# Attention of a two-layer decoder trunk: values become the weights of the product, key blocks are merged by the mask, the steps stand at other slots

## The chip, the cores and the metric

The kernel runs on one core of one Trainium2 chip. TensorE (PE) multiplies; a product loads one operand as weights (PEld) and streams the other past them, and the result lands in PSUM. VectorE (DVE), ScalarE (ACT) and GpSimd (POOL) work element by element; SyncE (SP) issues most DMAs. The metric is the device time of one execution in microseconds (us), lower is better.

## The reference, cut to what matters

Two layers work on 256 tokens of width 2048. In each, the normalised input is projected to queries, keys, values, u and v of a gating unit, and gate logits. The attention branch looks back over 127 earlier tokens, in blocks of 128:

```python
q_pos = jnp.arange(BLOCK)[:, None] + BLOCK
k_pos = jnp.arange(2 * BLOCK)[None, :]
diff = q_pos - k_pos
band = (diff >= 0) & (diff < WINDOW)          # WINDOW = BLOCK = 128
valid = (jnp.arange(nb)[:, None, None] > 0) | (k_pos >= BLOCK)[None]
...
scores = jnp.where(mask, scores, -1e30)
...
probs = jax.nn.softmax(jnp.concatenate([scores, sink], axis=-1), axis=-1)[..., :-1]
out = jnp.einsum('bnhgqk,bnkhd->bnqhgd', probs.astype(v.dtype), vw)
```

There are 16 query heads and 4 key heads (each serves 4 query heads), of 64 numbers each. A query at place i of its block sees of the block before only the keys at places above i, and of its own block only the keys up to i: each place counts in exactly one of the two blocks, so a query has 128 valid keys at most. The attention output is multiplied by `w_attn_branch`, the gating unit's by `w_sgu_branch`; both are gated, merged, multiplied by `w_out` and added to x, and a SwiGLU of width 5632 follows.

## The kernel before, in words

All large products are of one form. A chunk of weights, 256 rows by 512 columns, is loaded by SP into a `raw` buffer (five of them), ACT rounds it to `whi` (line 225), DVE subtracts to `wlo` (line 226), and PE takes three products for each pair of blocks, written to `acc` (lines 314 and 315). So a weight in fp32 goes through PE in parts that PE streams in one pass. Weights are rounded and subtracted four chunks ahead of PE.

The program is a list of such chunks. `tick()` moves a counter of slots on by one for each chunk or so (12 products of `acc`). `after(n, fn)` puts a step n slots later. PE's order is as written; the order on the other engines is arranged when the program is built.

The attention of a layer is in the class `Attention`. It runs between those products, while the projection is still going on:

- `keys` and `queries` normalise and rotate, and turn the result by DVE transposes of 32x32 blocks (`turn`, line 383), whose pieces SP then gathers by 16 DMAs of 32 KB (line 388).
- `scores(t, g)` (line 723) takes one block of 128 queries `t` and one key head `g`. It makes four products of 64 rows, in two PSUM tiles, for 128 keys (t = 0) or 256 keys (t = 1). DVE adds the mask (line 727), takes the maximum, ACT takes the exponential with the sum of each row.
- `weights(t, g)` (line 752), 5 slots later, turns the probabilities by PE, four transposes for each block of keys, and ACT takes them out of PSUM (line 754).
- `values(t, g)` (line 762), 3 slots later, takes the turned probabilities as the weights and streams 64 columns of values past them, for each head and each block of keys. DVE multiplies by the reciprocal of the sum (line 766) into `att`.
- `transposed` turns `att` in the way of `turn` (16 DMAs on SP) and splits it in two parts, `uh` and `ul`, for the product with `w_attn_branch`.

The scores of the first four heads-and-blocks stand 17, 22, 27 and 32 slots behind their queries, those of the second four at 29, 34, 39 and 44. PSUM tiles named `at` are two in number; scores (two tiles), values (one) and the gating unit's mixing product (`psg`, line 840) share them. Two more, `tr`, serve the transposes.

The gating unit's `v` (class `Spatial`) gets a GELU, its means taken off and is scaled, in steps from 1 to 9 slots behind each of its two chunks.

Of the kernel before, what the change touches and what calls it, by code (L numbers as in the profile page):

```python
# [15 lines left out]
NT = 2  # L16
# [41 lines left out]
def hybrid_trunk(ctx: ExitStack, tc: tile.TileContext, x, mix_norm, w_in, q_norm, k_norm, sinks,  # L58
# [92 lines left out]
    plans = []  # L151
    for l in range(DEPTH):
        wl = w_in[l]

        def of_in(kind, c):
            o = {"kv": O_KV, "q": 0, "v": O_V, "u": O_U, "gate": O_GATE}[kind] + c * CW
            return wl[:, o:o + CW]

        for f in FIRST_PART[l]:
            plans.append((single if len(f) == 1 else pair)(("in", l), *(of_in(*c) for c in f)))  # L160
        plans += [single(("att", l), w) for w in cols_of(w_attn_branch[l], NCH)]
# [26 lines left out]
    class Stream:  # L188
# [7 lines left out]
        def load(self, upto):  # L196
            while self.asked < min(upto, len(entries)):
                for key, w, h, tag in entries[self.asked]["loads"]:
                    raw = wraw.tile([P, 2, CW], F32, tag=tag, name=nm("raw"), bufs=None if tag == "raw" else 1)
                    src = w[2 * h * P:2 * (h + 1) * P, :].rearrange("(k p) n -> p k n", p=P)  # L200
                    if self.raws:
                        self.loaded = nc.sync.dma_start(raw, src)
                    else:
                        for i in range(2):
                            self.loaded = nc.sync.dma_start(raw[:, i:i + 1], src[:, i:i + 1])
                    self.raws[key] = raw
                self.asked += 1

# [317 lines left out]
    for c in range(NCH):  # L526
# [1 line left out]
    after(7, lambda: norm.finish())  # L528
    after(10, lambda: norm.unit(WINO, again=True))

    mask = const.tile([P, S], F32, name="mask")
    nc.gpsimd.memset(mask, 0.0)
    nc.gpsimd.affine_select(mask[:, :P], mask[:, :P], pattern=[[1, P]], base=0, channel_multiplier=-1,
                            compare_op=ALU.is_gt, fill=-1e30)
    nc.gpsimd.affine_select(mask[:, P:], mask[:, P:], pattern=[[-1, P]], base=0, channel_multiplier=1,
                            compare_op=ALU.is_ge, fill=-1e30)
    cs = const.tile([P, NT, HD // 2], F32, name="cs")
    sn = const.tile([P, NT, HD // 2], F32, name="sn")
    nc.gpsimd.dma_start(cs, cosine.rearrange("(t p) h -> p t h", p=P))
# [92 lines left out]
    def fetch_large(pl):  # L632
        for n, i in ((13, 2), (17, 3), (21, 0), (25, 1)):
            after(n, lambda i=i: pl.fetch(i))
        after(40, pl.spatial)

    class Attention:


        def __init__(self, pl):  # L640
            self.pl = pl
            self.qT = [None] * 2
            self.att = [None] * 2
            self.attT = [None] * 2
            self.live = {}

        def rotate(self, src, n, rope, outs):

# [35 lines left out]
        def keys(self, kv):  # L684
# [2 lines left out]
            self.rotate(kv[:, :, :KVW], NKV, self.pl.rope[1], [kd[:, :, :, j, :] for j in range(2)])  # L687
            self.kT = slot([P, 4, NKV, NT, B], name="kT")
            after(K_TURN, lambda: turn(self.kT, kd.rearrange("p t n a d -> p t (n a d)"), nc.sync))

        def queries(self, c, q):
            self.rotate(q, NQ // 2, self.pl.rope[0], None)
            self.qT[c] = slot([P, 4, S], name="qT")
            self.att[c] = slot([P, NT, CW], name="att")
# [18 lines left out]

        def scores(self, t, g):
            nk = P * (t + 1)
            mk = mask[:, P:] if t == 0 else mask
            snk, nsnk = self.pl.snk, self.pl.nsnk
            pr = slot([P, 2, 2, S], name="pr")
            for j in range(2):
                pscore = ps_at.tile([P, 2, S], F32, tag="at", name=nm("psc"))  # L720
                for i in range(2):
# [5 lines left out]
                nc.vector.tensor_tensor(out=pr[:, :, j, :nk], in0=pscore[:, :, :nk],  # L727
                                        in1=mk.unsqueeze(1).to_broadcast([P, 2, nk]), op=ALU.add)
            pr4 = pr.rearrange("p i j k -> p (i j) k")
            mx = tiny(4, "mx")  # L730
            nc.vector.tensor_reduce(out=mx, in_=pr4[:, :, :nk], axis=AX.X, op=ALU.max)
# [5 lines left out]
            nc.scalar.activation(es, es, AF.Exp)  # L737
            den = tiny(4, "den")
            for h in range(4):
                nc.scalar.activation(pr4[:, h, :nk], pr4[:, h, :nk], AF.Exp, bias=nm_[:, h:h + 1],  # L740
                                     accum_out=den[:, h:h + 1])
# [3 lines left out]
            after(5, lambda: self.weights(t, g, pr4, rd))  # L745

        def weights(self, t, g, pr4, rd):
            pT = []
            for kb in range(t + 1):
                pt = ps_tr.tile([P, 4, P], F32, tag="tr", name=nm("ppt"))  # L750
                for h in range(4):
                    nc.tensor.transpose(pt[:, h, :], pr4[:, h, kb * P:(kb + 1) * P], ident)  # L752
                pT_ = temp((P, 4, P), "pT")
                nc.scalar.activation(pT_, pt, AF.Copy)
                pT.append(pT_)
            after(3, lambda: self.values(t, g, pT, rd))

        def values(self, t, g, pT, rd):
            po = ps_at.tile([P, 4, HD], F32, tag="at", name=nm("po"))
            for h in range(4):  # L760
                for kb in range(t + 1):
                    nc.tensor.matmul(po[:, h, :], pT[kb][:, h, :],  # L762
                                     self.kv[:, kb, KVW + g * HD:KVW + (g + 1) * HD],
                                     start=kb == 0, stop=kb == t)
            o = (g % 2) * 256
            nc.vector.tensor_tensor(out=self.att[g // 2][:, t, o:o + 256].rearrange("p (h d) -> p h d", d=HD),
                                    in0=po, in1=rd.unsqueeze(2).to_broadcast([P, 4, HD]), op=ALU.mult)

    class Spatial:

# [236 lines left out]
```

## Time and profile before

| what | value |
| --- | --- |
| median of 3 runs | 2474.78 us (2472.15 to 2475.66) |
| the profiled execution | 2473.06 us |
| its span in the profile | 2471.1 us |
| busy: PE, PEld, DVE, ACT, POOL | 99%, 82%, 78%, 58%, 11% |
| granted clock of TensorE | 1.00 |
| DMA, mean | 203 GB/s |

The page gives busy time per engine, the chain of work that ended last, and the costliest groups of instructions (line, engine, operation, tile written and read, shape, count, busy time, mean duration of one, idle time before and what ended it). A matmul's duration includes its way through the array, so that durations of neighbours overlap: what a product costs is read from the distance between starts in the timeline. An fp32 product that isn't split appears as two instructions of PE, a transpose as one.

### The profile page before, as it was taken

What the parts mean: (1) busy time and instruction counts of PE and PEld (TensorE: products, weight loads), DVE (VectorE), ACT (ScalarE), POOL (GpSimd) and SP (SyncE); (2) the same over time, 40 slices, a digit from 0 to 9 for tenths busy, and PEclk for the clock granted to TensorE, in tenths of its full rate; (3) what the DMA queues carried; (4) which work ended last, traced back from release to release, by engine and by line L of the source; (5) the groups of instructions that cost most, each with busy time, mean ns of one, the idle gap of its engine ahead of it and who ended that gap; (6) DMA issues with size and microseconds to landing.
All of it is one profiled execution on the core that took longest, in us unless ns stands there. A gap on an engine that the chain in (4) does not pass through costs nothing.

```text
span 2471.1 us, 31179 instructions
## 1 busy us (share of the span) xinstructions
PE 2456.6 (99%) x11088; PEld 2032.1 (82%) x11088; DVE 1925.3 (78%) x2261; ACT 1430.8 (58%) x1794; POOL 283.2 (11%) x527
## 2 busy tenths in 40 slices
PE   9999999999999999999999999999999999999999
PEld 7888888888888888888887888888888888888887
DVE  6798676887877787778887986767878777877786
ACT  5566544575655565556655665545655555655564
POOL 3100002231110111011101000021211001110110
PEclk9999999999999999999999999999999999999999
DMA  9655667576766667576757546666767566666664
GB/s 293 203 181 163 214 200 218 182 241 190 220 197 204 214 195 223 175 228 188 227 153 265 154 155 224 208 209 188 231 188 233 189 215 195 218 198 202 213 196 148
DMA packets 275662, 502.54 MB, mean 203 GB/s; under 512 B 26225, under 2 KB 36049, under 8 KB 275505
## 3 DMA queue, kind: packets, MB, share of 16 engines
q1 hardware_dynamic: 259472, 484.25, 61.8%
q0 software_dynamic: 15712, 16.01, 2.2%
q8 instruction: 87, 1.43, 0.2%
q14 instruction: 71, 0.57, 0.1%
q10 hardware_dynamic: 320, 0.27, 0.0%
HBM read 475.27 MB, written 2.10 MB: 193 GB/s over the span
## 4 chain that ended last, share of the span: by engine, by line
PE 94%; DVE 2%; DMA 1%; SPq 1%; issue 1%; ACT 0%; POOL 0%; DVEq 0%; ACTq 0%
PE acc L314 61%; PE acc L315 30%; DMA raw<-in_w_in_dram 1%; SPq L388 1%; DVE wlo L226 1%; PE po L762 1%; PE pt L425 1%; PE ppt L752 0%; PE psc L723 0%; ACT whi L225 0%; PE psg L840 0%; DVE box L383 0%; POOL rq L286 0%; DVE raw L213 0%; DVE gate L928 0%
## 5 line engine op out<-in xcount | busy, mean ns | idle before, releaser
L226 DVE TENSOR_TENSOR wlo<-raw,whi 128x1024 fp32r<-128x1024 f32 (+1 forms) x1039 | 1260.7, 1219 | 493.7 <-ACT whi L225 485.1
L225 ACT ACTIVATE whi<-raw 128x1024 fp32r<-128x1024 f32 (+1 forms) x1039 | 1098.2, 1058 | 919.4 <-PE acc L315 720.9
L314 PE MATMUL acc<-whi,uh 128*128 128x512 f32 x3114 | 1217.9, 391 | 1.2 <-ACT uh L411 1.2
L314 PE MATMUL acc<-wlo,uh 128*128 128x512 f32 x3114 | 1214.0, 390 | 2.2 <-DVE wlo L226 2.2
L315 PE MATMUL acc<-whi,ul 128*128 128x512 f32 x3114 | 1213.5, 390 | 0.0
L314 PEld LDWEIGHTS acc<-wlo,uh 128*128 128x128 f32 x3114 | 585.1, 188 | 124.9 <-DVE wlo L226 5.0
L314 PEld LDWEIGHTS acc<-whi,uh 128*128 128x128 f32 x3114 | 585.1, 188 | 121.7 <-ACT uh L411 1.8
L315 PEld LDWEIGHTS acc<-whi,ul 128*128 128x128 f32 x3114 | 584.9, 188 | 121.7 <-DVE ul L416 0.2
L388 POOL DMA_DIRECT2D tt<-box x480 | 235.2, 497 | 1714.9 <-DVE box L383 784.1
L213 DVE TENSOR_TENSOR raw<-raw,raw 128x1024 f32<-128x1024 f32 x188 | 229.2, 1219 | 1.3
L314 PE MATMUL acc<-whi,sh 128*128 128x512 f32 x376 | 147.3, 392 | 0.0
L314 PE MATMUL acc<-wlo,sh 128*128 128x512 f32 x376 | 147.1, 391 | 0.0
L315 PE MATMUL acc<-whi,sl 128*128 128x512 f32 x376 | 146.5, 390 | 0.0
L315 PEld LDWEIGHTS acc<-whi,sl 128*128 128x128 f32 x376 | 70.6, 188 | 14.7
L314 PEld LDWEIGHTS acc<-wlo,sh 128*128 128x128 f32 x376 | 70.7, 188 | 14.6 <-DVE kept L339 0.4
L314 PEld LDWEIGHTS acc<-whi,sh 128*128 128x128 f32 x376 | 70.7, 188 | 14.3
L339 DVE TENSOR_TENSOR kept<-acc,kept 128x512 f32<-128x512 f32 x94 | 64.2, 684 | 0.0
L342 ACT ACTIVATE acc<-kept 128x512 f32<-128x512 f32 x94 | 55.1, 587 | 10.8 <-DVE kept L339 10.7
L857 DVE SCALAR_TENSOR_TENSOR xs<-acc,xs 128x512 f32<-128x512 f32 (+1 forms) x66 | 41.4, 666 | 7.8 <-PE acc L315 7.8
L946 ACT ACTIVATE hid<-acc,rhalf 128x512 f32<-128x512 f32 x44 | 30.4, 690 | 21.0 <-PE acc L315 21.0
L947 DVE SCALAR_TENSOR_TENSOR hid<-hid,acc 128x512 f32<-128x512 f32 x44 | 29.6, 683 | 8.3 <-ACT hid L946 8.3
L336 ACT ACTIVATE kept<-acc 128x512 f32<-128x512 f32 x47 | 28.0, 597 | 13.2 <-PE acc L315 13.2
(135 smaller groups left out, 880.5 us busy)
## 6 DMA issues: line engine op xcount, KB each, us to landing
raw<-in_w_in_dram SPq DMA_DIRECT2D x239, 512.0 KB, 4.7
raw<-in_w_up_dram SPq DMA_DIRECT2D x176, 512.0 KB, 4.8
raw<-in_w_gate_dram SPq DMA_DIRECT2D x176, 512.0 KB, 4.3
raw<-in_w_down_dram SPq DMA_DIRECT2D x176, 512.0 KB, 4.6
raw<-in_w_out_dram SPq DMA_DIRECT2D x64, 512.0 KB, 4.8
raw<-in_w_attn_branch_dram SPq DMA_DIRECT2D x32, 512.0 KB, 5.3
raw<-in_w_sgu_branch_dram SPq DMA_DIRECT2D x32, 512.0 KB, 4.3
tt<-box POOLq DMA_DIRECT2D x480, 32.0 KB, 4.2
```

The source lines that it names most:

```text
L213: self.last = nc.vector.tensor_tensor(out=self.raws[d], in0=self.raws[x], in1=self.raws[y], op=ALU.subtract)
L225: nc.scalar.activation(hi[:, i, :], raw[:, i, :], AF.Copy)
L226: self.last = nc.vector.tensor_tensor(out=lo[:, i, :], in0=raw[:, i, :], in1=hi[:, i, :].bitcast(F32), op=ALU.subtract)
L314: nc.tensor.matmul(ps, a, part[:, kk, :], start=first and kk + n == 0, stop=False, skip_group_check=True)
L315: nc.tensor.matmul(ps, b, hi[:, kk, :], start=False, stop=kk == 1, skip_group_check=True)
L336: nc.scalar.activation(p.kept[:, 1, :], a[0], AF.Copy)
L339: nc.vector.tensor_tensor(out=p.kept[:, int(tag == "P7"), :], in0=a[1], in1=p.kept[:, 1, :], op=ALU.add)
L342: nc.scalar.activation(ps, p.kept[:, t, :], AF.Copy)
L388: queue.dma_start(dst[j * B:(j + 1) * B, i], box[i * B:(i + 1) * B, j])
L857: nc.vector.scalar_tensor_tensor(out=xs[:, t, sl], in0=sums[t][:, i * w:(i + 1) * w], scalar=scale, in1=xs[:, t, sl], op0=ALU.mult, op1=AL ...
L946: nc.scalar.activation(th, g[t], AF.Tanh, scale=norm.rh[t])
L947: nc.vector.scalar_tensor_tensor(out=th, in0=th, scalar=1.0, in1=g[t], op0=ALU.add, op1=ALU.mult)
```

## The change

- `scores`: the block of 256 keys becomes 128. For t = 1 ACT copies the scores of the own block, and DVE writes the scores of the block before over them where the mask says so (`copy_predicated`). Maximum and exponential work on 128 keys. The buffer `pr` is of another pool (five buffers that it shares with short-lived work of the GELU and others).
- The probabilities are multiplied by the reciprocal of their sum on DVE, 4 slots behind the scores, 128x512 at a time.
- `weights`: four transposes for either t, 7 slots behind the scores. For t = 1 DVE makes a second copy in which only the keys of the own block are kept (`causal`).
- `values(t, c)`: one step for two key heads. The values are the weights (64 columns), and 512 columns of probabilities stream past them; the two key heads write to partitions 0 to 63 and 64 to 127. For t = 1 the two products of a head are: all probabilities with the values of the block before, and the kept ones with the difference of the two blocks' values, which DVE makes once per layer. The result has the channels in the partitions already: ACT and DVE split it into `uh` and `ul` straight out of PSUM, and `att`, its DVE transposes and its DMAs are gone.
- The rows of `w_attn_branch` are loaded in the order in which the heads now lie: two DMAs over 64 partitions in the place of one over 128.
- Slots: scores at 15, 19, 23, 27 and 31, 36, 41, 46; values 10 slots behind the second score of their pair; the second `v` chunk's GELU and scaling 10 slots later; the transposes of the spatial weights at slot 34 in the place of 40.

```diff
-Q_FIRST = 17
-Q_STEP = 5
+W_TURN = 7
+V_LATE = 0, 10
+SCORES = (15, 19, 23, 27), (31, 36, 41, 46)
...
+    def rows_of(raw, w, h):
+
+        if w.shape[0] != QW or not any(w is a for a in by_heads):
+            return [(raw, w[2 * h * P:2 * (h + 1) * P, :].rearrange("(k p) n -> p k n", p=P))]
+        rows = w.rearrange("(c a k d) n -> c a d k n", c=2, a=2, d=HD)
+        k = 2 * (h % 2)
+        return [(raw[a * HD:(a + 1) * HD], rows[h // 2, a, :, k:k + 2]) for a in range(2)]
...
-        after(40, pl.spatial)
+        after(34, pl.spatial)
...
+            after(K_TURN, lambda: nc.vector.tensor_tensor(out=kv[:, 0, :KVW], in0=kv[:, 1, KVW:], in1=kv[:, 0, KVW:],
+                                                          op=ALU.subtract))
...
-            n = Q_FIRST + (4 * Q_STEP - 8) * c
             for t in range(NT):
-                for g in (2 * c, 2 * c + 1):
-                    after(n, lambda t=t, g=g: self.scores(t, g))
-                    n += Q_STEP
-            after(n + 6, lambda: transposed(self.attT, c, self.att[c], queue=nc.sync))
+                for i in range(2):
+                    after(SCORES[c][2 * t + i], lambda t=t, g=2 * c + i: self.scores(t, g))
+                after(SCORES[c][2 * t + 1] + W_TURN + 3, lambda t=t: self.values(t, c))
...
-                nc.vector.tensor_tensor(out=pr[:, :, j, :nk], in0=pscore[:, :, :nk],
-                                        in1=mk.unsqueeze(1).to_broadcast([P, 2, nk]), op=ALU.add)
+                mk = mask.unsqueeze(1).to_broadcast([P, 2, P])
+                if t == 0:
+                    nc.vector.tensor_tensor(out=pr[:, :, j, :], in0=pscore[:, :, :P], in1=mk, op=ALU.add)
+                else:
+                    nc.scalar.activation(pr[:, :, j, :], pscore[:, :, P:], AF.Copy)
+                    nc.vector.copy_predicated(pr[:, :, j, :], mk.bitcast(mybir.dt.uint32), pscore[:, :, :P])
...
+            after(4, lambda: nc.vector.tensor_tensor(out=pr4, in0=pr4, in1=rd.unsqueeze(2).to_broadcast([P, 4, P]),
+                                                     op=ALU.mult))
+            after(W_TURN, lambda: self.weights(t, g, pr4))
...
-            for h in range(4):
-                for kb in range(t + 1):
-                    nc.tensor.matmul(po[:, h, :], pT[kb][:, h, :],
-                                     self.kv[:, kb, KVW + g * HD:KVW + (g + 1) * HD],
-                                     start=kb == 0, stop=kb == t)
...
+            po = ps_at.tile([P, 4, P], F32, tag="at", name=nm("po"))
+            pT = self.pT[t, c]
+            for k in range(t + 1):
+                for a in range(2):
+                    v = (1 - k) * KVW + (2 * c + a) * HD
+                    nc.tensor.matmul(po[a * HD:(a + 1) * HD], self.kv[:, 0, v:v + HD], pT[k][:, a],
+                                     start=k == 0, stop=k == t)
+            uh, ul = (x[:, :, t * P:(t + 1) * P] for x in units)
+            nc.scalar.activation(uh, po, AF.Copy)
+            nc.vector.tensor_tensor(out=ul, in0=po, in1=uh.bitcast(F32), op=ALU.subtract)
...
-                after(1 + t, lambda t=t: self.gelu(vt, t))
-                after(4 + 3 * t, lambda t=t: self.center(c, t))
+                after(V_LATE[c] + 1 + t, lambda t=t: self.gelu(vt, t))
+                after(V_LATE[c] + 4 + 3 * t, lambda t=t: self.center(c, t))
```

More of the change, by code (lines that the diff above doesn't have):

```diff
@@ L149, in pair @@
         return Plan(key, head, body)
-    plans = []
+    plans, by_heads = [], []
     for l in range(DEPTH):
@@ L160, in hybrid_trunk @@
             plans.append((single if len(f) == 1 else pair)(("in", l), *(of_in(*c) for c in f)))
-        plans += [single(("att", l), w) for w in cols_of(w_attn_branch[l], NCH)]
+        by_heads += cols_of(w_attn_branch[l], NCH)
+        plans += [single(("att", l), w) for w in by_heads[-NCH:]]
         sgu = [single(("sgu", l), w_sgu_branch[l, :, j * CW:(j + 1) * CW]) for j in range(NCH)]
@@ L199, in load @@
                     raw = wraw.tile([P, 2, CW], F32, tag=tag, name=nm("raw"), bufs=None if tag == "raw" else 1)
[L200 to L205, printed above, removed]
+                    for dst, src in rows_of(raw, w, h):
+                        if self.raws:
+                            self.loaded = nc.sync.dma_start(dst, src)
+                        else:
+                            for i in range(2):
+                                self.loaded = nc.sync.dma_start(dst[:, i:i + 1], src[:, i:i + 1])
                     self.raws[key] = raw
@@ L529, in hybrid_trunk @@
     after(10, lambda: norm.unit(WINO, again=True))
-    mask = const.tile([P, S], F32, name="mask")
+    mask = const.tile([P, P], F32, name="mask")
     nc.gpsimd.memset(mask, 0.0)
-    nc.gpsimd.affine_select(mask[:, :P], mask[:, :P], pattern=[[1, P]], base=0, channel_multiplier=-1,
-                            compare_op=ALU.is_gt, fill=-1e30)
-    nc.gpsimd.affine_select(mask[:, P:], mask[:, P:], pattern=[[-1, P]], base=0, channel_multiplier=1,
+    nc.gpsimd.affine_select(mask, mask, pattern=[[-1, P]], base=0, channel_multiplier=1,
                             compare_op=ALU.is_ge, fill=-1e30)
+    causal = const.tile([P, P], F32, name="causal")
+    nc.gpsimd.memset(causal, 1.0)
+    nc.gpsimd.affine_select(causal, causal, pattern=[[1, P]], base=0, channel_multiplier=-1, compare_op=ALU.is_ge, fill=0.0)
     cs = const.tile([P, NT, HD // 2], F32, name="cs")
@@ L642, in __init__ @@
             self.qT = [None] * 2
-            self.att = [None] * 2
             self.attT = [None] * 2
-            self.live = {}
+            self.pT, self.out = {}, {}
         def rotate(self, src, n, rope, outs):
@@ L693, in queries @@
             self.qT[c] = slot([P, 4, S], name="qT")
-            self.att[c] = slot([P, NT, CW], name="att")
+            self.attT[c] = None
             after(Q_TURN, lambda: self.turn_queries(c, q))
-            n = Q_FIRST + (4 * Q_STEP - 8) * c
             for t in range(NT):
-                for g in (2 * c, 2 * c + 1):
-                    after(n, lambda t=t, g=g: self.scores(t, g))
-                    n += Q_STEP
-            after(n + 6, lambda: transposed(self.attT, c, self.att[c], queue=nc.sync))
+                for i in range(2):
+                    after(SCORES[c][2 * t + i], lambda t=t, g=2 * c + i: self.scores(t, g))
+                after(SCORES[c][2 * t + 1] + W_TURN + 3, lambda t=t: self.values(t, c))
         def turn_queries(self, c, q):
@@ L715, in scores @@
             nk = P * (t + 1)
-            mk = mask[:, P:] if t == 0 else mask
             snk, nsnk = self.pl.snk, self.pl.nsnk
-            pr = slot([P, 2, 2, S], name="pr")
+            pr4 = temp((P, 4, P), "pr")
+            pr = pr4.rearrange("p (i j) k -> p i j k", j=2)
             for j in range(2):
@@ L726, in scores @@
                                      start=True, stop=True)
[L727 to L729 removed]
+                mk = mask.unsqueeze(1).to_broadcast([P, 2, P])
+                if t == 0:
+                    nc.vector.tensor_tensor(out=pr[:, :, j, :], in0=pscore[:, :, :P], in1=mk, op=ALU.add)
+                else:
+                    nc.scalar.activation(pr[:, :, j, :], pscore[:, :, P:], AF.Copy)
+                    nc.vector.copy_predicated(pr[:, :, j, :], mk.bitcast(mybir.dt.uint32), pscore[:, :, :P])
             mx = tiny(4, "mx")
[L731 removed]
+            nc.vector.tensor_reduce(out=mx, in_=pr4, axis=AX.X, op=ALU.max)
             nm_ = tiny(4, "negm")
@@ L744, in scores @@
             nc.vector.reciprocal(out=rd, in_=den)
-            after(5, lambda: self.weights(t, g, pr4, rd))
-        def weights(self, t, g, pr4, rd):
-            pT = []
-            for kb in range(t + 1):
-                pt = ps_tr.tile([P, 4, P], F32, tag="tr", name=nm("ppt"))
-                for h in range(4):
[L752 to L756, printed above, removed]
@@ L758, in values @@
-        def values(self, t, g, pT, rd):
-            po = ps_at.tile([P, 4, HD], F32, tag="at", name=nm("po"))
-            for h in range(4):
-                for kb in range(t + 1):
-                    nc.tensor.matmul(po[:, h, :], pT[kb][:, h, :],
-                                     self.kv[:, kb, KVW + g * HD:KVW + (g + 1) * HD],
-                                     start=kb == 0, stop=kb == t)
-            o = (g % 2) * 256
-            nc.vector.tensor_tensor(out=self.att[g // 2][:, t, o:o + 256].rearrange("p (h d) -> p h d", d=HD),
-                                    in0=po, in1=rd.unsqueeze(2).to_broadcast([P, 4, HD]), op=ALU.mult)
+            after(4, lambda: nc.vector.tensor_tensor(out=pr4, in0=pr4, in1=rd.unsqueeze(2).to_broadcast([P, 4, P]),
+                                                     op=ALU.mult))
@@ new lines, in scores, with weights @@
+            after(W_TURN, lambda: self.weights(t, g, pr4))
+        def weights(self, t, g, pr4):
+            if g % 2 == 0:
+                self.pT[t, g // 2] = [slot([P, 2, 4, P], name="pT") for _ in range(t + 1)]
+            pT = self.pT[t, g // 2]
+            pt = ps_tr.tile([P, 4, P], F32, tag="tr", name=nm("ppt"))
+            for h in range(4):
+                nc.tensor.transpose(pt[:, h, :], pr4[:, h, :], ident)
+            nc.scalar.activation(pT[0][:, g % 2], pt, AF.Copy)
+            if t == 1:
+                nc.vector.tensor_tensor(out=pT[1][:, g % 2], in0=pt, in1=causal.unsqueeze(1).to_broadcast([P, 4, P]),
+                                        op=ALU.mult)
@@ new lines, in values @@
+        def values(self, t, c):
+            if t == 0:
+                self.out[c] = slot([P, 4, S], F32R, "uh"), slot([P, 4, S], F32R, "ul")
+            units = self.out[c]
+            po = ps_at.tile([P, 4, P], F32, tag="at", name=nm("po"))
[8 more added lines that the diff above has]
+            nc.vector.tensor_tensor(out=ul, in0=po, in1=uh.bitcast(F32), op=ALU.subtract)
+            if t == NT - 1:
+                self.attT[c] = units
```

2 lines of the change are left out of this document (1 added, 1 removed).

## The prediction

> **What bounds the kernel now.** I read the page first: busy times, then the chain that ended last.
>
> ```profile
> span 2471.1 us, 31179 instructions
> PE 2456.6 (99%) x11088; PEld 2032.1 (82%) x11088; DVE 1925.3 (78%) x2261; ACT 1430.8 (58%) x1794; POOL 283.2 (11%) x527
> PE 94%; DVE 2%; DMA 1%; SPq 1%; issue 1%; ACT 0%; POOL 0%; DVEq 0%; ACTq 0%
> ```
>
> PE is busy all the way, so only what takes time on PE, or makes it stand still, moves the end. Next the groups by form and two windows, one over each layer's attention.
>
> ```profile
> L314 PE MATMUL acc<-whi,uh 128*128 128x512 f32 x3114 | 1217.9, 391 | 1.2 <-ACT uh L411 1.2
> L762 PE MATMUL po<-kv,pT 128*128 128x64 f32 x192 | 23.1, 270 | 0.0
> L752 PE MATMUL ppt<-ident,pr 128*128 128x128 f32 x96 | 13.8, 280 | 2.1 <-DVE wsT L623 2.1
> ...
> 95.00:250.00 155.00, 154.66 (x784) 127.08 (x783) 130.89 (x223) 101.83 (x183) 9.93 (x6) 1.00 0.57 178
> 1330.00:1485.00 155.00, 152.13 (x771) 125.27 (x770) 129.14 (x221) 102.52 (x182) 5.79 (x4) 1.00 0.54 173
> ```
>
> PE works through 154.66 and 152.13 of 155 us (first column after the length), DVE 131 and 129 (third). The large products of `acc` are not touched; the change can win what the small groups between them take, some tens of us in all, and the 2.9 us by which the second window is less full. Busy times overlap, so I price a group by starts: first `acc` behind it, less last `acc` ahead, less the 0.23 at which `acc` products follow each other, plus what the next product is late.
>
> ```profile
> 142.72 0.39 PE L315 MATMUL acc<-whi,sl 128*128 128x512 f32 x1
> 142.95 1.00 PE L762 MATMUL po<-kv,pT 128*128 128x64 f32 x8
> 143.76 0.48 PE L314 MATMUL acc<-whi,uh 128*128 128x512 f32 x1
> 144.07 0.39 PE L314 MATMUL acc<-wlo,uh 128*128 128x512 f32 x1
> ...
> 1395.27 0.39 PE L315 MATMUL acc<-whi,ul 128*128 128x512 f32 x1
> 1395.50 1.89 PE L762 MATMUL po<-kv,pT 128*128 128x64 f32 x16
> 1397.20 0.48 PE L314 MATMUL acc<-whi,uh 128*128 128x512 f32 x1
> 1397.52 0.39 PE L314 MATMUL acc<-wlo,uh 128*128 128x512 f32 x1
> ...
> 233.56 0.40 PE L315 MATMUL acc<-whi,ul 128*128 128x512 f32 x1
> 233.79 1.04 PE L752 MATMUL ppt<-ident,pr 128*128 128x128 f32 x8
> 234.58 0.48 PE L314 MATMUL acc<-whi,uh 128*128 128x512 f32 x1
> 234.90 0.40 PE L314 MATMUL acc<-wlo,uh 128*128 128x512 f32 x1
> ...
> 249.89 0.39 PE L315 MATMUL acc<-whi,ul 128*128 128x512 f32 x1
> 250.12 1.02 PE L840 MATMUL psg<-v,wsT 128*128 128x256 f32 x4
> 250.79 0.58 PE L314 MATMUL acc<-whi,uh 128*128 128x512 f32 x1
> 251.21 0.40 PE L314 MATMUL acc<-wlo,uh 128*128 128x512 f32 x1
> ```
>
> Values, t = 0: 143.76 - 142.72 - 0.23 = 0.81, and 0.31 - 0.23 = 0.08 behind, 0.89 us. Values, t = 1: 1.70 + 0.09 = 1.79. Eight transposes: 0.79 + 0.09 = 0.88. The mixing product: 0.67 + 0.19 = 0.86 for four instructions of 256 columns, so 0.215 each; an fp32 product is two instructions, and one of 512 columns takes 0.43.
>
> **The values on PE.** Before, 16 groups (two t, four g, two layers): 8 x 0.89 + 8 x 1.79 = 21.4 us. After, 8 groups (t, c). Each has two column tiles; per block of keys each tile streams 512 columns in two instructions, 2 x 0.43 = 0.86 us. Whether the two tiles run side by side decides the case, and no row shows column tiles. The nearest are the scores, whose two PSUM tiles use the upper and the lower 64 rows of the array:
>
> ```profile
> 149.10 0.39 PE L315 MATMUL acc<-whi,ul 128*128 128x512 f32 x1
> 149.42 1.14 PE L723 MATMUL psc<-kT,qT 64*128 64x256 f32 x8
> 150.49 1.09 PE L752 MATMUL ppt<-ident,pr 128*128 128x128 f32 x8
> ```
>
> Eight instructions of 256 columns would take 1.72 us in a row (0.215 each); they took 1.07, which is four times 0.215 and 0.21. The halves run side by side, though the code gives all of one tile ahead of the other. I take the same for columns. The switch costs 0.09 on the way in (0.32 for 0.23); the 0.21 holds the first weights and the way out; 0.09 behind it makes 0.39. So t = 0: 0.39 + 0.86 = 1.25, t = 1: 0.39 + 1.72 = 2.11; 4 x 3.36 = 13.4 us. Gain 8.0. Bounds: no overlap, 4 x (0.39 + 1.72 + 0.39 + 3.44) = 23.8, a loss of 2.4; overlap without switching cost, 4 x 2.58 = 10.3, a gain of 11.1.
>
> **Transposes.** For t = 1 four fall away in each of 8 groups: half of 0.88, so 3.5 us. **Breaks.** Score and transpose groups shared 18 breaks in `acc`; in the order of the built program they have 30 (the slots 7 behind no longer coincide with the next scores). Twelve more at 0.09: -1.1. The scores on PE stay as they are.
>
> **Standing still.** Two waits of PE lie in the second window:
>
> ```profile
> 1351.06 0.72 PE L723 MATMUL psc<-kT,qT 64*128 64x128 f32 x8
> 1353.93 0.66 PE L752 MATMUL ppt<-ident,pr 128*128 128x128 f32 x4 [2.15 <-DVE wsT L623]
> ...
> 1414.26 1.89 PE L762 MATMUL po<-kv,pT 128*128 128x64 f32 x16
> ...
> 1417.52 0.71 PE L723 MATMUL psc<-kT,qT 64*128 64x128 f32 x4
> 1418.94 0.71 PE L723 MATMUL psc<-kT,qT 64*128 64x128 f32 x4 [0.71 <-DVE att L766]
> ```
>
> First: a transpose waits 2.15 until DVE has emptied the spatial weights' tile. After, these weights stand at slot 34 and the next transposes 3 slots (36 products, some 8 us) or more behind them: gain 2.2. Second: the scores' second tile waits for the values' tile, emptied late; the two tiles start 1.42 apart instead of together. This pair moves apart: gain 1.4.
>
> The built order makes a new one of that kind, once in each layer: the values (t = 0, c = 1) stand directly ahead of the last scores (36 + 7 + 3 and 46 behind their queries: one slot). The scores' second tile then needs the buffer that the values have just filled. Emptying now goes through two engines in turn:
>
> ```profile
> 1418.47 0.42 DVE L766 TENSOR_TENSOR att<-po,rd 128x256 f32<-128x256 f32 x1
> ...
> L754 ACT ACTIVATE pT<-ppt 128x512 f32<-128x512 f32 x24 | 13.3, 588 | 4.2 <-PE ppt L752 4.2
> L408 DVE TENSOR_TENSOR ul<-tt,uh 128x512 fp32r<-128x512 f32 x44 | 28.9, 684 | 3.1 <-ACT uh L407 3.1
> L727 DVE TENSOR_TENSOR pr<-psc,mask 128x512 f32<-128x512 f32 x16 | 10.8, 681 | 2.1 <-PE psc L723 2.1
> L731 DVE TENSOR_REDUCE mx<-pr 128x4 f32<-128x1024 f32 x8 | 9.6, 1205 | 0.0
> L383 DVE STREAM_TRANSPOSE box<-att 128x512 f32<-128x512 f32 x8 | 5.6, 704 | 0.0
> ...
> 106.09 10.46 SPq L388 DMA_DIRECT2D tt<-box  x16
> raw<-in_w_attn_branch_dram SPq DMA_DIRECT2D x32, 512.0 KB, 5.3
> ```
>
> At best ACT 0.59 and DVE 0.68, 1.3 us. As at 1418.47, where DVE came to it late: values over at 1416.15 (1414.26 and 1.89), emptied at 1418.89, 2.7 later, and ACT's 0.59 on top: 3.3. The scores lose all of it, since the first tile alone, then the second alone, take what both took together twice. Middle 2.3, twice: -4.6 (2.6 to 6.6). One more handover, values (t = 1, c = 0) to scores in layer 1, is one slot apart (12 products, 2.7 us): 0 to 3, I take -0.5.
>
> **DVE and ACT** (shapes priced by the rows above: 128x512 0.68, 128x256 0.42). DVE loses 16 mask additions of 0.68 (10.8), half of 8 maxima (4.2 if a maximum goes by size), 16 `att` (6.7), 8 transposes (5.6), 8 `ul` (5.5): 32.8 us. It gains 16 predicated copies (no row; 0.42 by size, 0.68 if the mask costs as much as data: 6.7 to 10.9, I take 0.42), 16 multiplications and 8 kept copies and 8 `ul` of 0.68 (21.8), two differences (0.8): 29 to 34. Even. ACT has 8 copies of 0.59 fewer, shorter exponentials, and 16 new copies: even too. On PE this is worth nothing as long as `wlo` stays four chunks ahead; DVE is idle for 24 and 26 us of the windows. If that cover went, a late chunk would hold PE by about one `wlo`.
>
> **Queues.** SP issues 64 gathers fewer, four bursts of 10.5 us in which no weights are asked for; 32 loads become 64 half loads. At 10.46 / 16 = 0.65 an issue that is 1.3 us per chunk of 12 products (2.7 us), and the landing of 5.3 is covered by the chunks ahead: nothing. Without cover, 32 x 0.65 = 21 us at most. POOL does one more fill and as many selects, early: nothing. The late `v` chunk is read by the mixing product some twenty slots on, and `pr` in the pool of five only delays ACT and DVE work with slots to spare: nothing, or a chunk's wait as above.
>
> **Sum:** -8.0 - 3.5 + 1.1 - 2.2 - 1.4 + 4.6 + 0.5 = -8.9 us. Against the profiled execution 2473.06 - 8.9 = 2464.2; the median of the runs lies 1.7 above it, so 2466.
>
> **Rivals.**
> - Half overlap (0.12): the second tile's first instruction may start only with the first tile's second one. Three steps of 0.43 for two at t = 0, five for four at t = 1: 8 x 0.43 = 3.4 more, 2469. The scores' 1.07 speaks against it: in that order they would take seven steps, 1.5 us. [...]
> - No overlap (0.13): 23.8 for 13.4, 10.4 more, 2476: within 0.2%.
> - Slower (0.10): two engines must now empty each `at` tile. If each of the 22 other handovers (16 scores, 8 values, less the two) held PE as at 1418.94, by 0.71, 15.6 us come on top: 2482. It decides against the change from 13.6 / 22 = 0.62 us each. Against it: nearly all stand three or four slots (8 to 11 us) apart.
> - The new wait doesn't show (0.10): 2466 - 4.6 = 2461.
>
> **How the numbers follow.** The forecast has 0.55, with its own range 2461 to 2471 (waits 2.6 to 9.6; overlap with less switching). A run of this kernel tells 0.2%, 5 us, from no change: faster means below 2469.8, slower above 2479.7. Faster: nine tenths of 0.55, the last rival, half of the first: 0.65. Slower: 0.10 and a little of no overlap, 0.12. The rest, 0.23, is the same. The range leaves out the slower case and the edges: 2460 to 2476.
>
> **What would show it.** Values: 8 groups, between starts 1.2 and 2.1 us; 1.9 and 3.6 would be no overlap, 1.6 and 2.5 half. `ppt` x64. No wait for `wsT`. A wait of a `psc` for `ul` or `uh` of 1 to 4 us at the last scores of each layer. DVE busy within 5 us of 1925. Wrong it would be if `acc` waited for `wlo` or `whi` in the windows, or if the loads of `w_attn_branch` landed late.

## The result, and the profile after

The changed kernel takes 2484.14 us (median; 2482.55 to 2484.92), the kernel before on the same chip 2472.59 (2471.43 to 2475.66): ratio 1.0044, interval 1.0034 to 1.0053. It is slower by 11.5 us; the forecast was 8.9 us faster. The profiled execution took 2484.66, against 2473.06 before.

The page of the changed kernel: span, busy times, and the chain that ended last by engine.

```profile
span 2482.9 us, 30816 instructions
PE 2454.7 (99%) x10912; PEld 2013.2 (81%) x10912; DVE 1924.6 (78%) x2263; ACT 1426.8 (57%) x1802; POOL 287.8 (12%) x528
PE 93%; DVE 4%; issue 1%; ACT 1%; DMA 1%; SPq 0%; POOL 0%; DVEq 0%; ACTq 0%
```

PE has 176 matmuls fewer and is busy for 1.9 us less, and the span is 11.8 us longer. So PE stands still for longer: span less busy time is 28.2 us, where it was 14.5. DVE's total is the same as before (1925.3). In the chain DVE went from 2% to 4%. Where PE stands is told by the waits of PE (in total, times, longest):

```profile
PE psc L733 <- DVE ul L787: 5.7, 2, 2.9
PE psc L733 <- ACT qT L717: 4.3, 1, 4.3
...
PE ppt L768 <- DVE pr L758: 2.3, 1, 2.3
PE acc L324 <- DVE kept L349: 1.9, 2, 1.4
PE acc L324 <- DVE wlo L236: 1.4, 5, 0.5
PE po L783 <- DVE pr L742: 1.4, 1, 1.4
PE ppt L768 <- ACT whi L235: 1.2, 1, 1.2
```

Before, such waits in attention came to 2.1 (`wsT`) and 0.7 us (`att`); both are gone. In their place stand 4.3 for `qT`, 5.7 for `ul`, 2.3 and 1.4 for `pr`, 1.2 for `whi` and 1.9 for `kept`, 16.8 us together. The 1.2 are put down to `whi`, which ACT ended last (1402.98), but the multiplication that these transposes read ended only at 1402.95: it is another wait for `pr`, of 3.5 us in all with the 2.3.

The two windows over the layers' attention, then short windows of 3.41 us around three of the waits. Columns: length, busy PE, PEld, DVE, ACT and POOL (with counts), granted clock, DMA share, GB/s.

```profile
95.00:250.00 155.00, 147.12 (x660) 114.81 (x659) 126.77 (x220) 96.71 (x183) 12.31 (x6) 0.97 0.52 168
1330.00:1485.00 155.00, 145.77 (x667) 113.11 (x666) 126.59 (x221) 98.04 (x184) 8.78 (x5) 0.99 0.51 166
...
97.50:100.91 3.41, 0.37 (x3) 0.38 (x4) 2.23 (x3) 1.06 (x2) 1.11 (x1) 1.00 0.42 97
100.91:104.32 3.41, 3.41 (x12) 2.77 (x12) 3.34 (x6) 1.15 (x2) 0.00 (x0) 0.50 1.02 389
...
227.20:230.62 3.42, 0.62 (x3) 0.19 (x2) 3.42 (x6) 0.68 (x2) 0.00 (x0) 1.00 0.68 204
230.62:234.03 3.41, 3.30 (x7) 2.27 (x8) 2.99 (x8) 0.38 (x1) 0.00 (x0) 0.50 0.71 231
234.03:237.44 3.41, 3.41 (x9) 2.64 (x9) 1.12 (x6) 2.69 (x10) 0.60 (x1) 0.50 0.08 7
...
1466.25:1469.66 3.41, 0.75 (x3) 0.67 (x4) 3.38 (x7) 0.34 (x2) 0.00 (x0) 1.00 0.79 262
1469.66:1473.07 3.41, 3.41 (x9) 2.27 (x8) 2.12 (x5) 1.31 (x6) 0.00 (x0) 0.50 0.13 48
```

PE was busy for 154.66 and 152.13 of 155 us before; now 147.12 and 145.77, and in these some products lie at half the clock. Behind the wait of the first scores (layer 0) and those of the last scores (one in each layer) the granted clock is 0.50, for 3.41, 6.82 and 3.41 us. Before, it was 1.00 in both windows.

The timeline at the places that matter: the values of t = 1, the first scores, the last scores of the first layer, and the transposes in the second layer.

```profile
88.43 10.01 SPq L398 DMA_DIRECT2D tt<-box  x16
95.82 0.39 PE L325 MATMUL acc<-whi,ul 128*128 128x512 f32 x1
99.85 1.15 ACT L717 ACTIVATE qT<-tt 128x512 f32<-128x512 f32 x2 [5.26 <-DMA tt<-box]
100.54 1.62 PE L733 MATMUL psc<-kT,qT 64*128 64x128 f32 x8 [4.33 <-ACT qT L717]
...
171.59 0.39 PE L325 MATMUL acc<-whi,ul 128*128 128x512 f32 x1
171.91 1.94 PE L783 MATMUL po<-pT,kv 128*64 128x512 f32 x8
173.78 0.50 PE L324 MATMUL acc<-whi,uh 128*128 128x512 f32 x1
174.12 0.40 PE L324 MATMUL acc<-wlo,uh 128*128 128x512 f32 x1
...
225.68 1.08 PE L783 MATMUL po<-pT,kv 128*64 128x512 f32 x4
226.69 1.13 PE L733 MATMUL psc<-kT,qT 64*128 64x256 f32 x4
228.85 1.22 DVE L236 TENSOR_TENSOR wlo<-raw,whi 128x1024 fp32r<-128x1024 f32 x1
229.99 0.68 DVE L787 TENSOR_TENSOR ul<-po,uh 128x512 fp32r<-128x512 f32 x1
230.73 2.07 PE L733 MATMUL psc<-kT,qT 64*128 64x256 f32 x4 [2.90 <-DVE ul L787]
...
1451.97 0.15 DVE L757 RECIPROCAL rd<-den 128x4 f32<-128x4 f32 x1
1455.88 0.69 DVE L758 TENSOR_TENSOR pr<-pr,rd 128x512 f32<-128x512 f32 x1
1456.63 0.66 PE L768 MATMUL ppt<-ident,pr 128*128 128x128 f32 x4 [2.31 <-DVE pr L758]
```

- First scores: SP has issued the gather of the queries by 98.44 (88.43 + 10.01), ACT waits for its last piece and copies from 99.85, and PE, done at 96.21, stands until 100.54.
- Last scores: the values end at 226.76, ACT and then DVE have to empty their tile; ACT is done at 227.50 (`uh`), but DVE reaches `ul` only at 229.99, behind a `wlo`.
- Transposes: the reciprocal is there at 1452.12, but DVE comes to the multiplication only at 1455.88, 3.8 us later; PE waits for it.

### The profile page after: what moved, and what is told of

Same layout as the page of the kernel before. It is cut to its first block, busy times and chain, and to the rows that moved or that the text cites. A ratio compares the mean times of both kernels' runs of the same rounds, so it can differ in the third digit from the quotient of the medians.

```text
span 2482.9 us, 30816 instructions
## 1 busy us (share of the span) xinstructions
PE 2454.7 (99%) x10912; PEld 2013.2 (81%) x10912; DVE 1924.6 (78%) x2263; ACT 1426.8 (57%) x1802; POOL 287.8 (12%) x528
## 4 chain that ended last, share of the span: by engine, by line
PE 93%; DVE 4%; issue 1%; ACT 1%; DMA 1%; SPq 0%; POOL 0%; DVEq 0%; ACTq 0%
PE acc L324 61%; PE acc L325 30%; DVE wlo L236 2%; DMA raw<-in_w_in_dram 1%; PE pt L435 1%; ACT whi L235 0%; DVE raw L223 0%; PE psc L733 0%; SPq L398 0%; PE po L783 0%; PE psg L862 0%; DVE v L838 0%; PE ppt L768 0%; DVE kept L349 0%; DVE bst L826 0%
## 5 line engine op out<-in xcount | busy, mean ns | idle before, releaser
L296 POOL TENSOR_TENSOR rv<-ve,neg_half 128x4 f32<-128x4 f32 x8 | 15.3, 1909 | 237.1 <-DVE ve L830 185.8
```

## The experiments

The theories named in the expectations. **A**: PE stands at three places (first scores of layer 0, last scores of each layer), and behind each the clock is halved. **B**: the emptying of the values' tile by two engines hurts everywhere. **C**: the half loads of `w_attn_branch` come late. **D**: the multiplication by the reciprocal, which now lies between scores and transposes in DVE's queue, comes too late for PE. **E**: DVE has too much work in these stretches wherever the steps stand.

**1. The first scores back to slot 17**, and the next to 20.

```diff
-SCORES = (15, 19, 23, 27), (31, 36, 41, 46)
+SCORES = (17, 20, 23, 27), (31, 36, 41, 46)
```

> The changed kernel with the first chunk's scores at 17, 20, 23, 27 slots in the place of 15, 19, 23, 27. Theory A (PE stood still at three places, and TensorE's clock was halved behind each): the first scores of layer 0 find their turned queries ready, the wait of 4.3 us goes and with it 3.4 us at half clock (1.7 lost): about 2484.1 - 6 = 2478 us, and no clock of 0.5 near 100 us. Theory B (the new way of emptying and masking on ACT and DVE delays PE a little everywhere): within 1 us of 2484. Theory C (the loads of w_attn_branch in halves cost it): 2484.

2483.63 us; ratio to the kernel before 1.0037 (1.0024 to 1.0051). From the waits of PE:

```profile
PE ppt L768 <- DVE pr L758: 6.0, 3, 2.7
```

The wait for `qT` is gone, and with it the half clock near 100 us (0.50 for 3.41 us in the changed kernel). Yet no gain is clear of the noise (10.1 us above the kernel before, for 11.5): the transposes wait 6.0 in the place of 2.3 us for `pr`, `acc` 4.4 in the place of 1.9 for `kept`, and behind the last scores of the second layer the clock is halved for 6.83 in the place of 3.41 us. That these scores, later but closer together, press on DVE is a likely reason; no run shows it by itself.

**2. The last scores three slots later**, so that the values' tile is emptied before they need it.

```diff
-SCORES = (15, 19, 23, 27), (31, 36, 41, 46)
+SCORES = (15, 19, 23, 27), (31, 36, 41, 49)
```

> The changed kernel with the last scores of a layer at 49 slots in the place of 46, so that they no longer stand directly behind values. Theory A: two waits of 2.9 us go, with about 1 us each for scores that ran one tile after the other, and 6.8 and 3.4 us at half clock (5.1 lost): about 2484.1 - 12 = 2472 us, and no clock of 0.5 in these places. Theory B and C: within 1 us of 2484.

2480.0 us; 1.0023 (1.0013 to 1.0032).

```profile
PE ppt L768 <- DVE pr L758: 6.2, 2, 3.9
```

No scores wait for `ul` any more, and 5.0 us are won (6.5 above the kernel before, for 11.5); the transposes wait for `pr` for 6.2 us in the place of 2.3. The clock in the second layer is 1.00 now; in the first it is still halved (0.50) behind the first scores, and for 3.41 us behind the longer of these waits.

**3. Both together.**

```diff
-SCORES = (15, 19, 23, 27), (31, 36, 41, 46)
+SCORES = (17, 20, 23, 27), (31, 36, 41, 49)
```

> Both moves together. Theory A: clock 1.00 from start to end, 2484.1 - 18 = 2466 us, which is below the kernel before (2472.6) and is what the prediction's sum gave. Theory B and C: about 2484.

2477.87 us; 1.0017 (1.0008 to 1.0027).

```profile
PE ppt L768 <- DVE pr L758: 8.9, 3, 3.9
```

None of the three waits of A is left, and the kernel is still slower than before. A alone doesn't explain the result: the transposes now wait 8.9 us for the multiplication. The clock is halved in two other places, for 3.41 us each, behind the longest of these waits and behind one of `acc` for `kept` (2.1 us).

**4. The kernel before, with the first scores alone at slot 15.**

```diff
-            n = Q_FIRST + (4 * Q_STEP - 8) * c
...
-                    after(n, lambda t=t, g=g: self.scores(t, g))
+                    after(n - 2 * (n == Q_FIRST), lambda t=t, g=g: self.scores(t, g))
```

> The kernel before with only the first scores of each layer 2 slots earlier (15 for 17), nothing else changed. Theory A: PE waits about 4 us for the turned queries in layer 0 and then runs 3.4 us at half clock: 2472.6 + 6 = 2478 us. Theory B and C: 2472.6, no change, as the step is only moved.

2479.28 us, 5.8 more than the kernel before (2473.5); 1.0020 (1.0011 to 1.0030). Timeline and a window of this run:

```profile
100.97 1.65 PE L723 MATMUL psc<-kT,qT 64*128 64x128 f32 x8 [4.12 <-ACT qT L707]
...
98.95:105.78 6.83, 4.81 (x16) 3.91 (x17) 6.46 (x9) 2.21 (x3) 0.00 (x0) 0.50 0.85 296
```

Two slots earlier, without anything else of the change, cost a wait of 4.12 us and a half clock over 6.83 us. Two slots are 24 products, some 5.5 us; three quarters of them came back as a wait, so slot 17 had a slack of little over 1 us.

**5. The transposes 10 slots behind the scores**, with the first scores at 17 and 20.

```diff
-W_TURN = 7
+W_TURN = 10
-SCORES = (15, 19, 23, 27), (31, 36, 41, 46)
+SCORES = (17, 20, 23, 27), (31, 36, 41, 46)
```

> The kernel with the first scores at 17, 20, 23, 27 (the last at 46 as in the changed kernel), and the transposes 10 slots behind the scores in the place of 7, values with them (so the last scores stand 3 slots ahead of values). Theory D (the multiplication by the reciprocal now stands between scores and transposes, and DVE, full in these stretches, comes to it too late): the transposes' waits for it (6.0 us at 17, 20, 23, 27; 8.9 with both moves) go to under 1 us, the waits of scores behind values go too, the clock stays 1.00: about 2466 us. Theory E (DVE's work is too much in these stretches wherever the steps stand): the waits come back at other instructions, of the same sum: 2477 to 2484 us.

2465.4 us against 2473.63; 0.9967 (0.9955 to 0.9978): faster than before by 8.2 us.

```profile
PE acc L324 <- DVE kept L349: 4.1, 3, 1.9
PE acc L324 <- DVE wlo L236: 3.1, 5, 1.4
```

No transposes and no scores wait any more, and the clock is 1.00 throughout. The edit does two things: the multiplication has six slots in the place of three before the transposes read it, and the values, which follow the transposes by three slots, go from slot 46 to 49, behind the last scores. Experiment 3, in which the last scores are out of the way too, takes the second apart from the first: it stood 4.4 us above the kernel before, this one 8.2 below, so some 12.6 us go with the slack for the multiplication (D), the 8.9 us of waits and half clock among them.

**6. The multiplication on ACT**, on top of experiment 3.

```diff
-            after(4, lambda: nc.vector.tensor_tensor(out=pr4, in0=pr4, in1=rd.unsqueeze(2).to_broadcast([P, 4, P]),
-                                                     op=ALU.mult))
+            after(4, lambda: [nc.scalar.activation(pr4[:, h, :], pr4[:, h, :], AF.Copy, scale=rd[:, h:h + 1])
+                              for h in range(4)])
```

> The kernel with both moves (first scores at 17, 20, 23, 27, last at 49), with the multiplication by the reciprocal on ACT (four of 128x128 with the reciprocal as the scale) in the place of one of 128x512 on DVE, 16 of them. Theory D: the transposes no longer wait for DVE (8.9 us in both moves together) and ACT has the room: 2477.9 - 9 - 3 (half clock) = 2466 us. Theory E: DVE is relieved by 11 us as well, so some of it, about 2472. If ACT becomes late instead: waits for it, 2478 or more.

2468.98 us; 0.9980 (0.9970 to 0.9989), 9.0 us better than experiment 3, each against the kernel before on its chip.

```profile
PE ppt L768 <- ACT pr L758: 3.4, 2, 2.0
```

The wait of the transposes falls from 8.9 to 3.4 us with the same slots. DVE also has 16 multiplications less to do, so D and E both say so; experiment 10 tells them apart.

**7. The second `v` chunk not put off.**

```diff
-V_LATE = 0, 10
+V_LATE = 0, 0
```

> The changed kernel with the second v chunk's steps at their old slots (no 10 slots of delay). Theory D and E (DVE's fullness): the steps fall where c = 0's values and t = 1 scores lie, so other waits, and fewer at the last scores: 2480 to 2488 us. If the delay itself is what costs: about 2473.

2482.06 us; 1.0034 (1.0021 to 1.0047), an interval that overlaps that of the changed kernel (1.0034 to 1.0053). Its waits move (`pr` 4.6 in one piece, `ul` 2.7 in two), and their sum stays near: 15.5 us for 16.8.

**8. `w_attn_branch` in whole loads.** The rows then lie in the old order.

```diff
-        if w.shape[0] != QW or not any(w is a for a in by_heads):
+        if True:
```

> The changed kernel with the loads of w_attn_branch whole again (128 partitions, 512 KB, one DMA), so that the rows of the attention's projection meet the wrong channels: that part of the result is another. Theory C (half loads cost it): 2472.6. Theories A, D, E: no change, within 1 us of 2484.

2484.9 us; 1.0046 (1.0031 to 1.0061). DMA issues, with the time to landing last:

```profile
raw<-in_w_attn_branch_dram SPq DMA_DIRECT2D x32, 512.0 KB, 4.6
```

The half loads landed after 5.7 us, the whole ones after 4.6, and the time is the same: C is false.

**9. The transposes 10 slots behind the scores, and nothing else.**

```diff
-W_TURN = 7
+W_TURN = 10
```

> The changed kernel with the transposes 10 slots behind the scores in the place of 7 and nothing else: first scores still at 15, last at 46. It takes away the waits of transposes for the multiplication and (since values move to 49) the scores' wait behind values, and leaves the first scores' wait for the turned queries in layer 0. Theory D with A: 2465.4 and the first wait with its half clock, 4.3 + 1.7: 2471 us. Theory E: 2477 or more.

2468.02 us against 2472.5; 0.9979 (0.9970 to 0.9988).

```profile
PE psc L733 <- ACT qT L717: 4.4, 1, 4.4
```

Of the waits of scores and transposes only this one is left. Changing `W_TURN` alone takes the changed kernel from 11.5 us above the kernel before to 4.5 below it. The wait that is left makes the difference to experiment 5, which is 8.2 below: the first scores at slot 15 (with the next at 19) cost 3.7 us here, 5.8 in experiment 4, and 1.4 in experiment 1, where other waits took up the room. Each of these differences is good to 2 or 3 us.

**10. Experiment 5, and the multiplication on ACT as in 6.**

> First scores at 17, 20, 23, 27, transposes 10 slots behind, and the multiplication on ACT. Theory D: the transposes no longer wait for it in either form, so the engine hardly matters: 2465 us, within 2. Theory E: DVE relieved by 11 us takes away most of the 7.2 us that acc products still wait for DVE: 2460 us.

2459.21 us against 2472.5; 0.9939 (0.9924 to 0.9955). It is faster than both kernels, by 13.3 us than the one before.

```profile
PE acc L324 <- DVE wlo L236: 1.4, 3, 0.6
PE acc L324 <- DVE kept L349: 1.3, 1, 1.3
```

In experiment 5 no transpose waited for the multiplication, so nothing of D was left to win; the 5.1 us that are won still (8.2 to 13.3) come with the waits of `acc` for `kept` and `wlo`, which fall from 7.2 to 2.7 us. So E is true to that extent: part of DVE's lateness comes from how much it has to do, and not from where a step stands.

**11. The changed kernel, with PE kept busy while it stands.** Products of the identity with itself, whose result nobody reads: 20 before the first scores of layer 0, 13 between the two tiles of the last scores of each layer.

```diff
+        def idle(self, n):
+            pd = ps_tr.tile([P, P], F32, tag="tr", name=nm("pd"))
+            for i in range(n):
+                nc.tensor.matmul(pd, ident, ident, start=True, stop=True)
...
+            if (t, g, self.pl.l) == (0, 0, 0):
+                self.idle(20)
             for j in range(2):
+                if (t, g, j) == (1, 3, 1):
+                    self.idle(13)
```

> The changed kernel with idle products (identity by identity, 128x128 fp32, into a PSUM tile that nobody reads) put where PE stands still: 20 ahead of layer 0's first scores, 13 between the two tiles of each layer's last scores. The waits stay, PE is only kept going in them. Theory A's second half (the clock is halved because PE stood, and that is a price of its own): clock 1.00 in these three places, and the 13.7 us at half clock give back half of what PE did in them: 2484.1 - 6 = 2478 us, at least 2480. If the half clock costs nothing, or doesn't come from standing still: 2484 or more.

2478.3 us (2477.32 to 2479.72); 1.0020 (1.0012 to 1.0029). Windows over the three places, and two short ones in the second layer:

```profile
95.00:105.00 10.00, 10.00 (x69) 8.93 (x68) 7.78 (x9) 2.32 (x4) 2.90 (x1) 1.00 0.59 195
225.00:240.00 15.00, 15.00 (x80) 11.89 (x77) 13.00 (x26) 7.67 (x18) 0.60 (x1) 1.00 0.50 154
1455.00:1475.00 20.00, 20.00 (x101) 15.63 (x100) 12.62 (x25) 12.32 (x31) 0.00 (x0) 1.00 0.34 98
...
1447.56:1450.97 3.41, 1.22 (x6) 0.68 (x4) 3.41 (x7) 1.70 (x3) 1.52 (x1) 1.00 0.54 150
1450.97:1454.38 3.41, 3.29 (x10) 2.80 (x11) 3.41 (x6) 0.60 (x1) 0.93 (x1) 0.50 0.60 171
```

The scores start about as late as in the changed kernel (in the second layer because the idle products outlast the wait: `ul` is done at 1463.20, the second tile starts at 1465.23), but the clock stays at 1.00 in all three places, and 5.8 us are won. So the half clock has a price of its own. Its size is not exactly these 5.8: the wait of the values for `pr` (1.4 us) is gone as well, and 3.41 us of half clock stand anew in the second layer (last line).

## Why the prediction was wrong

Right were the parts that it worked out from what PE executes:

- **The values on PE** (2.11 us at t = 1 by full overlap): 173.78 - 171.59 - 0.23 = 1.96, and 0.34 - 0.23 = 0.11 behind, 2.07 us. At t = 0 (148.14) it is 1.20, for 1.25. The two column tiles run side by side, and both rivals with less overlap fall. Eight instructions of 512 columns over the same 128 rows took 1.94 us (171.91), where 0.43 each in a row would be 3.4; in all, half overlap, whose order of starts no row shows, was put at 2.5 us and no overlap at 3.6, for the 2.07 measured.
- **The predicated copy** (0.42 to 0.68 us), the transposes (64 of them) and the old wait for `wsT`, which went, came out as forecast, and DVE's total is even. The groups by form:

```profile
L742 DVE COPY_PREDICATED pr<-mask,psc 128x256 f32<-128x256 uint32 x16 | 6.8, 442 | 0.8 <-ACT pr L741 0.8
L768 PE MATMUL ppt<-ident,pr 128*128 128x128 f32 x64 | 9.7, 273 | 3.5 <-DVE pr L758 2.3 <-ACT whi L235 1.2
```

- **Loads**: free, as said (experiment 8).
- **The sum without waits.** The terms that are no waits of the new order (-8.0, -3.5, 1.1, -2.2, -1.4) make -14.0. Experiment 5 has every part of the change, at other slots. There `acc` waits for 9.2 us in all, 3.4 in the kernel before: -14.0 + 5.8 = -8.2, and -8.2 was measured. In experiment 10 `acc` waits for 3.6: -13.8, and -13.3 was measured. Each of the two is measured to 3 or 4 us. That experiment 5 also comes near the forecast of -8.9 is luck: the forecast has 5.1 us of waits of the scores, experiment 5 other waits of nearly the same size. This confirms the sum, and not each term.

Wrong were four steps: three on when something is ready, and one on what follows when it isn't.

- **"The scores on PE stay as they are."** The first ones moved from slot 17 to 15, and the step didn't ask when their queries come. A gather was priced, for SP's queue alone (the later one, at 106.09), and none was followed to its reader. The profile before has the answer:

```profile
88.20 10.01 SPq L388 DMA_DIRECT2D tt<-box  x16
99.64 1.15 ACT L707 ACTIVATE qT<-tt 128x512 f32<-128x512 f32 x2 [5.47 <-DMA tt<-box]
```

  The first scores stood at 101.16 there, just behind that copy. After the change `qT` is ready at about 100.5 again, and slot 15 comes at 96.2. Price 4.33 us of waiting; 5.8 in all by experiment 4.
- **The new wait at the last scores** was foreseen, 2.3 us each (2.6 to 6.6 for both). The waits came to 5.7, inside this range and above its middle, but the cost did not end there: the scores' tiles no longer run side by side (some 1 us each time), and the clock came on top. The step counted how long ACT and DVE work and one late arrival of DVE; here DVE came 3.2 us after the values' end (229.99 - 226.76), and only then took its 0.68.
- **"On PE this is worth nothing as long as `wlo` stays four chunks ahead"**, said of DVE's work. Busy totals were even, and `wlo` did hold (1.4 us of waiting, 2.2 before). But the multiplication by the reciprocal had changed its place: it used to follow the values on PE, and now PE's transposes wait for it. Three slots for a DVE that is busy for whole windows (3.42 of 3.42 at 227.20) are too few. In the changed kernel this shows as 3.5 us only; where the scores no longer wait it is 8.9 (experiment 3), and with three slots more it is nothing (experiments 5 and 9). That `pr` "only delays ACT and DVE work with slots to spare" trusts in the same slots; whether the pool of five delayed anything, no run shows.
- **The clock** had no term. The granted clock of the kernel before was 1.00, though it has a wait of 2.15 us, and the forecast kept it at that without a reason; the new stands are longer (4.33, 2.90 and 2.75 us). The trace has 0.50 in stretches of 3.41, 6.82 and 3.41 us behind them, and 1.00 in the next 3.42 us after each (104.32, 237.44, 1473.07). In the 3.41 us ahead of each stretch PE was busy for 0.37, 0.62 and 0.75 us (last section). At half clock products of `acc` follow each other at 0.43 us (233.75, 234.17) and not at 0.23; for the 13.5 us that PE was busy there, that is an estimate of 6.3 us. Experiment 11 measured 5.8, with the reservations said there.

The signs that the prediction gave for being wrong did not come: `acc` waited for `wlo` and `whi` for 1.4 and 0.5 us only, and the loads cost nothing. The time was lost at scores and transposes, where no sign was set but for the last scores.

The account, in spans (11.8 us longer): the sum without waits is -14.0. The waits of PE in the attention and at `acc` come to 19.6 us (the 16.8 above, `wlo` 1.4, `uh` 0.9, other `whi` 0.5), where `acc` waited for 3.4 before: 16.2 more. The half clock is 6.3, and the second tiles of the last scores, which run by themselves, are some 2 (an estimate from the first layer: the first tile takes 1.13, the second 232.73 - 230.73 = 2.00 at half clock or 1.0 at full, and both together took 1.07 before). That makes 10.5; 1.3 us stay without a row that names them.

The rival "slower" (2482) put its price on the emptying of `at` tiles by two engines at all 22 other handovers, 15.6 us. The size came near, the mechanism didn't: of those handovers one shows in the waits, where values wait for the scores' tile (`po` for `pr` of L742, 1.4 us at 1384.29). The handover that was priced at 0.5 (values to scores in the second layer, 1418.06) shows no wait.

## What to carry to other kernels

When a step is moved to an earlier slot, or a step is put between two that PE executes, ask for each new pair of neighbours when the operand is ready, with the queue ahead of it on its engine; a busy total that comes out even says nothing on that. Mending one wait at a time can look useless (experiment 1 won 1.4 us, where experiment 4 puts the step at 5.8), because the next one in the same queue takes its place; give the queue slack, or take work off it. A new stand of PE should be counted with what the clock can take behind it: in the changed kernel stands of 4.33, 2.90 and 2.75 us had 3.41, 6.82 and 3.41 us at half clock behind them, while 2.31 us there and 2.15 us in the kernel before had none.

## What the runs showed of the hardware that was not expected

**In the changed kernel the stretches at half clock start whole multiples of 3.413 us apart**: at 100.91, 230.62 and 1469.66; the second and third are 129.71 and 1368.75 us behind the first, 38 and 401 times 3.4133. In each case the window of that length just ahead is the one in which PE stood: busy for 0.37, 0.62 and 0.75 of 3.41 us. The length of a wait alone does not tell whether a half clock follows. A wait of 2.31 us for `pr` in the second layer had a stretch of 3.41 us at 0.50 behind it in experiment 11, where nearly all of it lay in the one window ahead of that stretch (PE busy for 1.22, quoted there). One of the same 2.31 us in the changed kernel had none; in windows counted from the starts above it lay over two:

```profile
1452.59:1456.01 3.42, 1.73 (x8) 1.11 (x6) 3.42 (x6) 2.20 (x4) 1.02 (x1) 1.00 0.42 125
1456.01:1459.42 3.41, 2.79 (x15) 2.39 (x16) 3.41 (x6) 0.60 (x1) 1.43 (x1) 1.00 0.67 214
```

**Nor does PE's busy time in the window ahead tell it.** In experiment 4 windows with 1.32 (95.54) and 1.40 us (98.95) of busy PE were followed by 0.50, and in the changed kernel one with 1.73 us (1452.59) by 1.00. But in experiment 4 one with 1.91 us was followed by 0.50 too:

```profile
6.79:10.20 3.41, 1.91 (x7) 0.92 (x6) 2.70 (x8) 3.40 (x9) 0.08 (x1) 1.00 1.09 342
10.20:13.62 3.42, 3.42 (x10) 2.54 (x10) 2.05 (x5) 1.46 (x4) 0.00 (x0) 0.50 0.95 275
```

In the changed kernel the window at 230.62, busy for 3.30 us at half clock, is followed by 0.50 again. What decides, no run shows. The stretch at 10.20 in experiment 4 lies ahead of anything that its edit moves; the changed kernel and experiment 11 have 1.00 there.

**The column tiles of the values, over the same 128 rows, ran side by side** as far as the times can tell: 2.07 us at t = 1 for eight instructions of 512 columns with both switches, where four of 0.43 make 1.72.
